# A written order for ScalarE and VectorE in the first stage of a transformer block kernel

## The chip, the cores and the metric

One core of a Trainium2 chip runs the whole program. The metric is device microseconds (us) of one execution; three executions of the kernel before gave 1308.18, 1308.55 and 1308.77 us. TensorE (PE in the profile) multiplies matrices into PSUM banks, ScalarE (ACT) and VectorE (DVE) work element by element, GpSimd (POOL) does a few small things, and DMA queues are fed by SyncE (SP), ScalarE and GpSimd.

## The reference

One layer of a hybrid block on 512 latent tokens of 2048 channels (256 context tokens beside them), all in float32:

```python
h = _modulate(_rmsnorm(xs, norm_g[l]), shift[:, None], scale[:, None])   # rmsnorm(x) * (1 + scale) + shift
p = h @ w_l                                   # 2048 -> 9216: q, k, v, z_a, u_b, z_b, g_a, g_b
q = _rope(_rmsnorm(_heads(p, OFF_Q, N_Q_HEADS), q_norm_g[l]), cos, sin) * q_scale
...
attn = _attention(q, jnp.concatenate([k, kc], axis=1), jnp.concatenate([v, vc], axis=1))
y_a = (attn * jax.nn.silu(z_a)) @ w_pa
y_b = (_fourier_mix(u_b) * jax.nn.silu(z_b)) @ w_pb
return (g_a * y_a + g_b * y_b) @ w_o          # then the gated residual and a last rmsnorm
```

`shift`, `scale` and `gate` are the product of `silu(c)` with `w_ada`. The change touches how `shift`, `scale` and `h` are made and how the first columns of `p` (u_b and z_b, 1024 of 9216) are computed beside that, and where two small tables for the rotations are loaded.

## The kernel before

Every float32 operand of a product is split into a high part `hi`, rounded to the format that TensorE multiplies fast, and the rest `lo`. ScalarE makes `hi` (a copy with rounding, L176) and VectorE `lo` (source minus `hi`, L177). One product is then three matmuls into the same bank: high weight by high row (L327), high weight by low row or the other way round (L328), and the remaining cross term (L329).

*The first stage* (0 to about 141 us) goes over the 2048 channels in 16 blocks of 128. x lies transposed, channel on partition, as `xt`. First the root of the mean square of every token: squares on ScalarE (L522, L526) or VectorE (L524), sums on VectorE (L527) and on TensorE (L528), root and reciprocal (L532, L533), and `spread` (L539), four fp32 products that put the reciprocals on all partitions. Then for each block k: `matvec`, 16 fp32 matmuls of `silu(c)` by a piece of `w_ada` (L551); ScalarE copies the result out (`ado`, L563); TensorE transposes it (L567); VectorE reduces it to columns (L576) and makes `gain` (L577) and `shift` (L579). `make_h` makes the row block: VectorE multiplies x by gain and reciprocal root (L592), ScalarE adds the shift and rounds to the high row (L593), VectorE makes the low row (L594). For k of 8 and above `form_row` makes three small VectorE results from blocks k and k-8 (L602 to L604), used in the second stage.

Beside this runs `start_work`, the products of the row blocks with the columns of u_b and z_b, as a generator that yields after each tile; `some(n)` lets it do n tiles. A piece covers one to four blocks and up to eight tiles of 128 columns. Tiles 0 to 3 stay in four banks named `pb` through the whole stage. Tiles 4 to 7 go to banks named `pc`, of which there are **two slots, used in turn**: a third `pc` tile can start only when the first has been taken out, the fourth when the second has. Taking out is `keep`: a ScalarE copy for block 0 (L611), otherwise the VectorE addition part <- pc + part (L613). The weights of the pieces come by SyncE's queue and are split by `split_next`.

What sets the order: TensorE's instructions stand in the order in which the code is written (`manual_schedule` for TensorE alone). For ScalarE and VectorE a scheduler chooses an order among ready work; `behind(ins)` only says that what stands inside it comes after `ins`. All engines run their own line in order.

*The turn to the second stage* (141 to about 178 us). The Fourier mixing of u_b takes `part` through `halves`, `channels`, `positions` and `gate_b`, and GpSimd writes the result to DRAM as `b_d` (two DMAs, L803). After that the remaining columns of `p` are computed by a seven-product scheme on weights that arrive as chains `R` (GpSimd's DMAs add to them, L280) and on forms of the rows (`S`, `Z`), again split by L176 and L177. The rotation tables `qr` (L1007 and L1008, `load_rotations`, issued by ScalarE) lie in the memory in which `part` lay, so their load has to wait until the `b_d` transfers are done; `rotations` multiplies them (L1013).

## Time and profile before

| what | value |
|---|---|
| three executions | 1308.18, 1308.55, 1308.77 us |
| profiled execution | 1308.72 us, span 1306.9 us, mean granted TensorE clock 0.998 |
| PE busy | 1278.5 us, 98% of the span |
| DVE, ACT, POOL busy | 993.8, 684.4, 166.4 us |
| chain that ended last | PE 78%, DVE 9%, DMA 6%, issue 3%, ACT 3% |

A timeline row reads: start, duration (both us from the start of the span), engine, line of the kernel, operation, output<-inputs, shapes, and in square brackets how long the engine had stood idle just before and what released it. A row of the windows view has the stretch, its length, busy time (and count) of PE, PE's weight loads, DVE, ACT and POOL, the granted TensorE clock, the share of the DMA engines in use and GB/s. A row of the waits view has the waiting engine and line, what it waited for, and total time, number and longest.

### The profile page before, as it was taken

What the parts mean: (1) busy time and instruction counts of PE and PEld (TensorE: products, weight loads), DVE (VectorE), ACT (ScalarE), POOL (GpSimd) and SP (SyncE); (2) the same over time, 40 slices, a digit from 0 to 9 for tenths busy, and PEclk for the clock granted to TensorE, in tenths of its full rate; (3) what the DMA queues carried; (4) which work ended last, traced back from release to release, by engine and by line L of the source; (5) the groups of instructions that cost most, each with busy time, mean ns of one, the idle gap of its engine ahead of it and who ended that gap; (6) DMA issues with size and microseconds to landing.
All of it is one profiled execution on the core that took longest, in us unless ns stands there. A gap on an engine that the chain in (4) does not pass through costs nothing.

```text
span 1306.9 us, 17539 instructions
## 1 busy us (share of the span) xinstructions
PE 1278.5 (98%) x6522; PEld 1046.7 (80%) x6522; DVE 993.8 (76%) x1296; ACT 684.4 (52%) x1080; POOL 166.4 (13%) x218
## 2 busy tenths in 40 slices
PE   7999999999999999999999999999999999999997
PEld 3676887888888888888888888888888888888885
DVE  4666889979788787657777766688898867887676
ACT  5222645555556455444354554666666646464554
POOL 0000011110202101011021020012110212221210
PEclk9999999999999999999999999999999999999999
DMA  9998486898899888976869897568872899998985
GB/s 384 351 367 345 169 235 160 252 235 267 211 269 261 253 292 257 323 212 180 265 202 266 300 227 248 180 214 247 245 238 81 234 254 239 248 214 230 220 205 170
DMA packets 103718, 318.54 MB, mean 244 GB/s; under 512 B 9808, under 2 KB 33104, under 8 KB 99280
## 3 DMA queue, kind: packets, MB, share of 16 engines
q1 hardware_dynamic: 54480, 197.86, 42.0%
q0 software_dynamic: 26544, 96.49, 34.6%
q10 hardware_dynamic: 22608, 23.07, 5.2%
q8 instruction: 51, 0.84, 0.2%
q14 instruction: 35, 0.29, 0.1%
HBM read 283.30 MB, written 34.09 MB: 243 GB/s over the span
## 4 chain that ended last, share of the span: by engine, by line
PE 78%; DVE 9%; DMA 6%; issue 3%; ACT 3%; SPq 0%; ACTq 0%; POOL 0%; DVEq 0%; POOLq 0%
PE banks L327 10%; PE banks L328 10%; PE banks L329 10%; PE x L329 7%; PE x L328 7%; PE x L327 6%; PE y L329 6%; PE y L327 6%; PE y L328 5%; DVE wlo L177 3%; PE banks L1371 2%; PE pd L551 2%; DMA wr<-in_w_g 2%; DMA wr<-in_ctx_toks 1%; DVE s L177 1%
## 5 line engine op out<-in xcount | busy, mean ns | idle before, releaser
L176 ACT ACTIVATE whi<-R 128x1024 fp32r<-128x1024 f32 x138 | 145.1, 1058 | 138.0 <-PE banks L329 49.1
L177 DVE TENSOR_TENSOR wlo<-R,whi 128x1024 fp32r<-128x1024 f32 x138 | 167.6, 1221 | 58.7 <-ACT whi L176 58.3
L177 DVE TENSOR_TENSOR wlo<-wr,whi 128x1024 fp32r<-128x1024 f32 (+1 forms) x122 | 147.2, 1212 | 65.0 <-ACT whi L176 64.8
L176 ACT ACTIVATE whi<-wr 128x1024 fp32r<-128x1024 f32 (+1 forms) x122 | 127.5, 1050 | 108.4 <-PE y L329 35.1
L327 PE MATMUL banks<-whi,s 128*128 128x512 f32 x396 | 157.2, 397 | 2.1 <-DVE ev L938 1.5
L329 PE MATMUL banks<-whi,s 128*128 128x512 f32 x396 | 155.2, 392 | 0.0
L328 PE MATMUL banks<-wlo,s 128*128 128x512 f32 x396 | 155.2, 392 | 0.0
L328 PE MATMUL x<-wlo,s 128*128 128x512 f32 x356 | 138.7, 390 | 0.3 <-DVE wlo L177 0.3
L327 PE MATMUL x<-whi,s 128*128 128x512 f32 x356 | 138.9, 390 | 0.0
L329 PE MATMUL x<-whi,s 128*128 128x512 f32 x356 | 138.7, 390 | 0.0
L328 PE MATMUL y<-wlo,s 128*128 128x512 f32 x308 | 120.2, 390 | 0.9 <-DVE wlo L177 0.9
L329 PE MATMUL y<-whi,s 128*128 128x512 f32 x308 | 119.9, 390 | 1.0 <-DVE s L177 1.0
L327 PE MATMUL y<-whi,s 128*128 128x512 f32 x308 | 120.2, 390 | 0.4 <-DVE cxe L1091 0.4
L280 POOL DMA_DIRECT2D R<-in_w_g x64 | 55.9, 873 | 423.3 <-DVE wlo L177 271.3
L176 ACT ACTIVATE s<-wr 128x512 fp32r<-128x512 f32 (+2 forms) x95 | 61.1, 676 | 72.1 <-DMA wr<-in_w_g 22.0
L177 DVE TENSOR_TENSOR s<-wr,s 128x512 fp32r<-128x512 f32 (+2 forms) x95 | 68.0, 747 | 34.1 <-ACT s L176 33.4
L327 PEld LDWEIGHTS banks<-whi,s 128*128 128x128 f32 x396 | 74.5, 188 | 17.6 <-ACT whi L176 1.9
L329 PEld LDWEIGHTS banks<-whi,s 128*128 128x128 f32 x396 | 74.4, 188 | 15.5
L328 PEld LDWEIGHTS banks<-wlo,s 128*128 128x128 f32 x396 | 74.5, 188 | 14.0 <-DVE wlo L177 0.2
L328 PEld LDWEIGHTS x<-wlo,s 128*128 128x128 f32 x356 | 66.9, 188 | 14.5 <-DVE wlo L177 0.7
L329 PEld LDWEIGHTS x<-whi,s 128*128 128x128 f32 x356 | 66.8, 188 | 13.8
L327 PEld LDWEIGHTS x<-whi,s 128*128 128x128 f32 x356 | 66.9, 188 | 13.7
(292 smaller groups left out, 2816.6 us busy)
## 6 DMA issues: line engine op xcount, KB each, us to landing
wr<-in_w_g SPq DMA_DIRECT2D x128, 512.0 KB, 5.2
wa<-in_w_ss SPq DMA_DIRECT2D x32, 1024.0 KB, 8.2
R<-in_w_g POOLq DMA_DIRECT2D x64, 512.0 KB, 6.9
R<-in_w_g SPq DMA_DIRECT2D x32, 512.0 KB, 5.8
wr<-in_w_gate SPq DMA_DIRECT2D x32, 512.0 KB, 5.2
wr<-in_w_o SPq DMA_DIRECT2D x24, 512.0 KB, 7.6
R<-in_w_o POOLq DMA_DIRECT2D x24, 512.0 KB, 9.2
wr<-in_w_pab SPq DMA_DIRECT2D x20, 512.0 KB, 5.7
```

Of the source, the lines that this page charges most:

```text
L176: first = nc.scalar.activation(hi, src, ACT.Copy)
L177: return first, nc.vector.tensor_tensor(lo, src, hi.bitcast(F32), op=ALU.subtract)
L280: nc.gpsimd.dma_start(chain[e.pc], e.nxt, accum_op=ALU.add)
L327: nc.tensor.matmul(o, ah, bh, start=start, stop=False, skip_group_check=cont)
L328: nc.tensor.matmul(o, ah, bl, start=False, stop=False, skip_group_check=cont)
L329: nc.tensor.matmul(o, al, bh, start=False, stop=stop, skip_group_check=cont)
L551: nc.tensor.matmul(acc[32 * j : 32 * j + 32], c2[:, n, :], w[:, k, :], start=n < 4, stop=n >= KK - 4)
L1371: nc.tensor.transpose(tp[:, k * P : (k + 1) * P], p[:, k * P : (k + 1) * P], ident)
```

## The change

1. For blocks 0 to 13 ScalarE and VectorE too run in the order in which the code is written; the last two blocks stay as they were, with `behind`. The squares get one more on VectorE (q=14).
2. Blocks 0 to 5 make the row another way. `by_root` forms y = x * reciprocal root before the columns are known; then ScalarE makes the high row straight from y with scale and shift (`row_hi`), and VectorE makes v = y * gain and the low row (`row_lo`). `hold` and `release` put one take-out of a bank between the two. Blocks 6 to 13 keep `make_h`.
3. Splits of weights are written ahead of the columns of a block, and in blocks 6 to 13 the take-outs of a block's `pc` tiles come where `some` stands in the code.
4. For one-block pieces with t = 0 the first two tiles do their four products with the high row first and those with the low row after them. `spread` stands between the halves of `matvec(0)`, and block 1's `matvec` comes after four tiles in place of two.
5. The first load of the rotation tables is issued by GpSimd; the second stays with ScalarE.

The diff; of the loops that are replaced only the new form is shown, since the old one stands in the kernel above:

```diff
@@ -520,7 +520,7 @@
             two = hm_tile([P, 2, T], F32, name=uid("sq"))
             a, b = two[:, 0, :], two[:, 1, :]
             nc.scalar.activation(a, xt[:, q, :], ACT.Square)
-            if q in (4, 8, 10):
+            if q in (4, 8, 10, 14):
                 nc.vector.tensor_tensor(b, xt[:, q + 1, :], xt[:, q + 1, :], op=ALU.mult)
             else:
                 nc.scalar.activation(b, xt[:, q + 1, :], ACT.Square)
@@ -554,10 +554,14 @@
 
     two = {}
 
-    def modulate(kb):
+    def modulate(kb, meanwhile=lambda: None):
         two[kb] = bank2()
         for h in range(2):
             matvec(kb, h)
+        meanwhile()
+        return taken(kb)
+
+    def taken(kb):
         o = o_of[kb] = pap.tile([P, 256], F32, tag="ada_o", bufs=2, name=uid("ado"))
         wada.pop(kb)
         return nc.scalar.copy(o, two[kb][:, :256])
@@ -570,7 +574,6 @@
         sp, o = two.pop(kb)[:, 256:], o_of.pop(kb)
         turned(sp, o)
         if kb == 0:
-            rx0.append(spread(*norms))
             warm(3, o)
         r = pap.tile([P, 2, 2], F32, tag="ada_r", bufs=2, name=uid("adr"))
         nc.vector.tensor_reduce(r, sp.rearrange("p (h g r) -> p h r g", h=2, g=4)[:, :, 0:2, :], axis=AX.X, op=ALU.add)
@@ -579,12 +582,26 @@
         last = nc.vector.tensor_scalar(shift[:, kb, :], r[:, 0, :], bada[:, kb : kb + 1], None, op0=ALU.add)
         return last
 
-    rx0 = []
+    rx0, y_of = [], {}
 
     def rows_of(kb):
         if kb % 2 == 0:
             pairs.append([hm_tile([P, 2, T], F32R, name=uid(n)) for n in ("hh", "hl")])
         hhi[kb], hlo[kb] = (t[:, kb % 2, :] for t in pairs[-1])
+
+    def by_root(kb):
+        y = y_of[kb] = whole["S3", 0][:, 2 * (kb % 2) : 2 * (kb % 2) + 2, :].rearrange("p a c -> p (a c)")
+        nc.vector.tensor_tensor(y, xt[:, kb, :], rx if kb else rx0[0], op=ALU.mult)
+
+    def row_hi(kb):
+        rows_of(kb)
+        nc.scalar.activation(hhi[kb], y_of[kb], ACT.Identity, bias=shift[:, kb, 0:1], scale=gain[:, kb, 0:1])
+
+    def row_lo(kb):
+        v = xt[:, kb, :]
+        nc.vector.tensor_scalar(v, y_of.pop(kb), gain[:, kb, 0:1], None, op0=ALU.mult)
+        nc.vector.scalar_tensor_tensor(hlo[kb], v, shift[:, kb, 0:1], hhi[kb].bitcast(F32),
+                                       op0=ALU.add, op1=ALU.subtract)
 
     def make_h(kb):
         rows_of(kb)
@@ -603,9 +620,12 @@
         nc.vector.tensor_tensor(whole["S3", h][:, i, :], a[:, :256], a[:, 256:], op=ALU.subtract)
         nc.vector.scalar_tensor_tensor(whole["Z5", h][:, i, :], a[:, 256:], d, b[:, 256:], op0=ALU.add, op1=ALU.subtract)
 
-    finals = []
+    finals, held = [], []
 
     def keep(t, acc, kb, nk):
+        if held and held[0] is None:
+            held[0] = t, acc, kb, nk
+            return
         dst = pt(t)
         if kb == 0 or t < 4:
             nc.scalar.copy(dst, acc)
@@ -624,6 +644,18 @@
                 order = [[(i, k)] for k in range(nk) for i in range(nt)]
             elif nt == 8:
                 order = [order[i] for i in TURNS]
+            if t == 0 and nk == 1:
+                both = [(i, sums_u[i] if i < 4 else bank3(), slice(P * i, P * i + P)) for (i, _), in order[:2]]
+                for i, acc, c in both:
+                    nc.tensor.matmul(acc, wh[:, 0, c], hhi[kb], start=kb == 0 or i > 3, stop=False, skip_group_check=i < 4)
+                    nc.tensor.matmul(acc, wl[:, 0, c], hhi[kb], start=False, stop=False, skip_group_check=i < 4)
+                for i, acc, c in both:
+                    nc.tensor.matmul(acc, wh[:, 0, c], hlo[kb], start=False, stop=i > 3, skip_group_check=i < 4)
+                    if i > 3:
+                        keep(i, acc, kb, nk)
+                order = order[2:]
+                yield 3
+                yield 3
@@ -658,65 +690,110 @@
...
+    def hold():
+        held[:] = [None]
+
+    def release():
+        k = held.pop()
+        keep(*k)
+
+    E = mybir.EngineType
+    with tc.manual_schedule(engines={E.PE}):
         norms = token_norms()
...
+        two[0] = bank2()
+        matvec(0, 0)
+        rx0.append(spread(*norms))
+        matvec(0, 1)
+        with tc.manual_schedule(engines={E.Activation, E.DVE}):
             split_next()
+            nc.scalar.copy(rx, rx0[0])
+            by_root(0)
+            taken(0)
+            wada[2] = wada_load(2)
+            load_start()
+            columns(0)
+            row_hi(0)
+            row_lo(0)
             split_next()
...
+            by_root(1)
+            some(4)
+            modulate(1, split_next)
+            wada[3] = wada_load(3)
+            load_start()
             some(2)
...
+            columns(1)
+            row_hi(1)
+            row_lo(1)
             some(2)
...
+            for kb in range(1, 4):
+                k = kb + 1
+                some(2)
+                by_root(k)
+                if kb > 1:
+                    split_next()
+                modulate(k)
+                if kb < 3:
+                    wada[k + 2] = wada_load(k + 2)
+                    load_start()
+                if kb == 1:
+                    split_next()
+                hold()
+                some(2)
+                columns(k)
+                row_hi(k)
+                release()
+                row_lo(k)
+                if kb == 3:
+                    some(2)
+                    by_root(5)
+                    modulate(5)
+                    for k in (6, 7):
+                        wada[k] = wada_load(k)
+                        load_start()
+                    hold()
+                    some(2)
+                    columns(5)
+                    row_hi(5)
+                    release()
+                    row_lo(5)
+                else:
+                    some(4)
+            for kb in range(4, KK - 4, 2):
+                some(3)
                 split_next()
...
+                for i in range(2):
+                    k = kb + 2 + i
+                    if i:
+                        some(3)
+                        split_next()
+                    modulate(k)
+                    if k + 2 < KK:
+                        wada[k + 2] = wada_load(k + 2)
+                        for _ in range(2 if k + 2 == KK - 3 else 1):
+                            load_start()
+                    some(2 - i)
+                    columns(k)
+                    make_h(k)
                     if k >= 8:
                         form_row(k - 8)
...
                 if kb == KK - 6:
                     split_table(0)
                     split_from(get(("dftc", 0)), fch[:, 0, :], fch[:, 1, :])
                     load_start()
+                some(3)
+        for i in range(2):
+            k = KK - 2 + i
+            some(2)
+            modulate(k)
+            some(2 - i)
+            columns(k)
+            ins = make_h(k)
+            with behind(ins):
+                split_next()
+                form_row(k - 8)
+            if not i:
+                load_start()
+        some(1)
         some(8)
     may[0], asks[0] = 1 << 30, nc.sync
     while next(work):
@@ -1003,9 +1080,9 @@
     new_q = lambda: qr[:, :1024].rearrange("p (a h d) -> p a h d", a=2, h=4)
     turning = qr[:, 1024:].rearrange("p (a t d) -> p a t d", a=2, t=4)
 
-    def load_rotations(rows):
-        nc.scalar.dma_start(turning, rope)
-        nc.scalar.dma_start(new_q()[:, 0, 0:2, :], rows)
+    def load_rotations(rows, q):
+        q.dma_start(turning, rope)
+        q.dma_start(new_q()[:, 0, 0:2, :], rows)
@@ -1216,7 +1293,7 @@
         qs[h] = take((2, T), F32R)
-    load_rotations(qkg[:, 0:2, :])
+    load_rotations(qkg[:, 0:2, :], nc.gpsimd)
@@ -1247,7 +1324,7 @@
                 with tc.issue_after(last_split[-1][1].ins):
                     rotations(HD ** -0.5)
             elif (g, name) == (KV, "P1"):
-                load_rotations(qkg[:, 2:4, :])
+                load_rotations(qkg[:, 2:4, :], nc.scalar)
             elif (g, name) == (KV, "Q5"):
                 with tc.issue_after(last_split[-1][1].ins):
                     rotations(1.0)
```

How instructions move, at three places. Names in a row are the program's, with the number of the buffer: `pc_` is a bank of the two turning slots, `adr` the reduced columns, `s_` here a low row being made, `wlo` a split of weights.

VectorE around the columns of block 9, before:

```order
L576 TENSOR_REDUCE adr_815<-pd_780 128x4
L577 TENSOR_SCALAR gain<-adr_815,bsc_98,small 128x2
L579 TENSOR_SCALAR shift<-adr_815,small 128x2
L592 SCALAR_TENSOR_TENSOR xt<-xt,gain,rx 128x512
L613 TENSOR_TENSOR part<-pc_830,part 128x512
L594 SCALAR_TENSOR_TENSOR s_759<-xt,shift,s_758 128x512
L602 TENSOR_TENSOR d_826<-shift 128x1
L603 TENSOR_TENSOR S_67<-xt 128x256
L177 TENSOR_TENSOR wlo_823<-wr_665,whi_822 128x1024
L604 SCALAR_TENSOR_TENSOR Z_69<-xt,d_826 128x256
L613 TENSOR_TENSOR part<-pc_838,part 128x512
L613 TENSOR_TENSOR part<-pc_846,part 128x512
```

and after the change:

```order
L579 TENSOR_REDUCE adr_823<-pd_788 128x4
L580 TENSOR_SCALAR gain<-adr_823,bsc_98,small 128x2
L582 TENSOR_SCALAR shift<-adr_823,small 128x2
L609 SCALAR_TENSOR_TENSOR xt<-xt,gain,rx 128x512
L611 SCALAR_TENSOR_TENSOR s_767<-xt,shift,s_766 128x512
L619 TENSOR_TENSOR d_830<-shift 128x1
L620 TENSOR_TENSOR S_67<-xt 128x256
L621 SCALAR_TENSOR_TENSOR Z_69<-xt,d_830 128x256
L633 TENSOR_TENSOR part<-pc_834,part 128x512
L633 TENSOR_TENSOR part<-pc_842,part 128x512
L633 TENSOR_TENSOR part<-pc_850,part 128x512
L177 TENSOR_TENSOR wlo_868<-wr_673,whi_867 128x1024
```

The first take-out of a bank behind the columns (pc_830 before, pc_834 now) moved from ahead of the low row (L594, now L611) to behind the low row and all three rows of `form_row`; the split of weights moved behind the take-outs. Blocks 7, 11 and 13 move in the same way; block 7 has no `form_row`, and at block 13 the splits `fsq` and `fch` stand ahead of the take-outs too.

VectorE around the columns of block 2, before:

```order
L613 TENSOR_TENSOR part<-pc_366,part 128x512
L576 TENSOR_REDUCE adr_373<-pd_338 128x4
L577 TENSOR_SCALAR gain<-adr_373,bsc_98,small 128x2
L579 TENSOR_SCALAR shift<-adr_373,small 128x2
L592 SCALAR_TENSOR_TENSOR xt<-xt,gain,rx 128x512
L613 TENSOR_TENSOR part<-pc_389,part 128x512
L613 TENSOR_TENSOR part<-pc_397,part 128x512
L594 SCALAR_TENSOR_TENSOR s_378<-xt,shift,s_377 128x512
L613 TENSOR_TENSOR part<-pc_405,part 128x512
```

and after the change:

```order
L594 TENSOR_TENSOR S_67<-xt,rx 128x512
L177 TENSOR_TENSOR wlo_365<-wr_235,whi_364 128x1024
L579 TENSOR_REDUCE adr_377<-pd_339 128x4
L580 TENSOR_SCALAR gain<-adr_377,bsc_98,small 128x2
L582 TENSOR_SCALAR shift<-adr_377,small 128x2
L633 TENSOR_TENSOR part<-pc_371,part 128x512
L602 TENSOR_SCALAR xt<-S_67,gain 128x512
L603 SCALAR_TENSOR_TENSOR s_382<-xt,shift,s_381 128x512
L633 TENSOR_TENSOR part<-pc_390,part 128x512
L633 TENSOR_TENSOR part<-pc_398,part 128x512
L633 TENSOR_TENSOR part<-pc_403,part 128x512
```

The product by the reciprocal root (L594, into S_67) stands ahead of the columns now, and a split of weights too. Of the three take-outs around the old low row (L594), one stands ahead of the new low row (L603) and three behind it.

ScalarE at the first load of the rotation tables, before:

```order
L176 ACTIVATE whi_1639<-R_1282 128x1024
L1007 DMA qr<-in_rope 128x1024
L1008 DMA qr<-in_qkg 128x256
L176 ACTIVATE s_1655<-Z_69 128x1024
L176 ACTIVATE whi_1660<-R_1279 128x1024
```

and after the change:

```order
L176 ACTIVATE whi_1648<-R_1287 128x1024
L176 ACTIVATE s_1664<-Z_69 128x1024
L176 ACTIVATE s_1686<-Z_70 128x1024
L176 ACTIVATE whi_1669<-R_1284 128x1024
L176 ACTIVATE s_1759<-S_67 128x1024
```

and GpSimd, after the change (before, the five rows are the same without the two of `qr`):

```order
L880 DMA b_d<-part 128x1024 x2
L1084 DMA qr<-in_rope 128x1024
L1085 DMA qr<-in_qkg 128x256
L280 DMA R_1284<-in_w_g 128x1024
L280 DMA R_1285<-in_w_g 128x1024
```

The two loads left ScalarE's line and stand in GpSimd's, between the writes of `b_d` and the additions to the weight chains `R`.

More of the change, by code (lines that the diff above doesn't have):

```diff
@@ L659, in split_next @@
         e.raws = []
-    with tc.manual_schedule(engines={mybir.EngineType.PE}):
-        norms = token_norms()
-        modulate(0)
-        wada[2] = wada_load(2)
-        load_start()
-        columns(0)
-        ins = make_h(0)
-        nc.scalar.copy(rx, rx0[0])
-        split_next()
-        with behind(ins):
-            split_next()
-            split_next()
-        for kb in range(4):
+    def hold():
[3 more added lines that the diff above has]
+        keep(*k)
@@ L674, in block_kernel @@
             some(2)
-            modulate(kb + 1)
-            if kb < 3:
-                wada[kb + 3] = wada_load(kb + 3)
-                load_start()
+            columns(1)
+            row_hi(1)
+            row_lo(1)
             some(2)
-            columns(kb + 1)
-            ins = make_h(kb + 1)
-            with behind(ins):
-                split_next()
-            if kb == 3:
-                some(2)
-                modulate(5)
-                for k in (6, 7):
-                    wada[k] = wada_load(k)
-                    load_start()
-                some(2)
-                columns(5)
-                make_h(5)
-            else:
-                some(4)
@@ L695, in block_kernel @@
-        for kb in range(4, KK - 2, 2):
-            n = 3 if kb < KK - 4 else 2
-            for i in range(2):
-                k = kb + 2 + i
-                some(n)
-                modulate(k)
-                if k + 2 < KK:
-                    wada[k + 2] = wada_load(k + 2)
-                    for _ in range(2 if k + 2 == KK - 3 else 1):
-                        load_start()
-                some(2 - i)
-                columns(k)
-                ins = make_h(k)
-                with behind(ins):
-                    split_next()
+            for kb in range(1, 4):
[31 more added lines that the diff above has]
+                    some(4)
@@ L710, in block_kernel @@
                     if k >= 8:
                         form_row(k - 8)
-                if k == KK - 2:
-                    load_start()
-            some(n - (n == 2))
-            with behind(ins):
                 if kb == KK - 6:
```

## The prediction

> **What bounds the kernel now.** I read the windows view first, by stage, then the waits of PE, then the timelines of PE and DVE at each place that the order of the changed kernel moves.

> ```profile
> 0.00:20.00 20.00, 11.51 (x48) 4.25 (x48) 10.10 (x22) 12.27 (x22) 1.89 (x11) 1.00 0.91 363
> 20.00:60.00 40.00, 36.49 (x279) 23.77 (x275) 22.69 (x42) 12.74 (x20) 0.00 (x0) 1.00 0.92 362
> 60.00:141.00 81.00, 80.40 (x590) 57.06 (x591) 52.43 (x109) 25.30 (x38) 0.00 (x0) 1.00 0.86 332
> 170.00:240.00 70.00, 67.32 (x292) 53.98 (x291) 64.28 (x76) 38.18 (x57) 9.73 (x12) 1.00 0.77 210
> ```

> PE sets the pace. From 20 to 60 us it stands idle 40.00 - 36.49 = 3.5 us, from 60 to 141 only 0.6, from 170 to 240 2.7. The granted clock is 1.00 throughout, so PE's work is neither longer nor shorter after the change: only its idle time can move. What the change can save is bounded by the first and the last of these; the long middle stretch has nothing to give and can only lose.

> ```profile
> PE pb L328 <- DVE s L594: 2.0, 4, 1.2
> PE pb L327 <- ACT s L593: 0.9, 2, 0.6
> ```

> These are the early waits: six times PE waits for a high row or for a low row of a new block.

> **The late blocks: where the change loses.** In blocks 7, 9, 11 and 13 VectorE's order changes from product, *take-out of a bank*, low row, ... to product, low row, the rows of `form_row`, *take-out*. PE's fourth `pc` tile after the transposes needs the slot that this take-out frees. First the price of being released by it, which block 13 shows already:

> ```profile
> 122.48 0.39 PE L329 MATMUL pc<-s,wlo 128*128 128x512 f32 x1
> 123.47 0.50 PE L327 MATMUL pc<-s,whi 128*128 128x512 f32 x1 [0.60 <-DVE part L613]
> ...
> 120.53 0.17 DVE L576 TENSOR_REDUCE adr<-pd 128x4 f32<-128x16 f32 x1
> 122.73 1.28 DVE L613 TENSOR_TENSOR part<-pc,part 128x512 f32<-128x512 f32 x2
> 125.99 1.22 DVE L177 TENSOR_TENSOR fsq<-wr,fsq 128x1024 fp32r<-128x1024 f32 x1
> 127.12 0.42 DVE L177 TENSOR_TENSOR fch<-wr,fch 128x256 fp32r<-128x256 f32 x1
> 127.46 1.22 DVE L177 TENSOR_TENSOR wlo<-wr,whi 128x1024 fp32r<-128x1024 f32 x1
> ```

> The take-out starts at 122.73 and PE, which had waited 0.60, goes on at 123.47, 0.74 after that start; its first matmul after a stop takes 0.50 and not 0.39, so a stop costs its wait and 0.1.

> Block 7, without `form_row`:

> ```profile
> 73.73 0.16 DVE L576 TENSOR_REDUCE adr<-pd 128x4 f32<-128x16 f32 x1
> 74.25 0.75 DVE L592 SCALAR_TENSOR_TENSOR xt<-xt,gain,rx 128x512 f32<-128x512 f32 x1
> 75.80 0.75 DVE L594 SCALAR_TENSOR_TENSOR s<-xt,shift,s 128x512 fp32r<-128x512 f32 x1 [0.20 <-ACT s L593]
> 76.47 0.68 DVE L613 TENSOR_TENSOR part<-pc,part 128x512 f32<-128x512 f32 x1
> 75.91 0.39 PE L327 MATMUL pc<-s,whi 128*128 128x512 f32 x1
> ```

> The low row waited for ScalarE (0.20), so it cannot start earlier when the take-out leaves its place ahead of it. The take-out then starts where the next instruction stood, 76.47, and PE's fourth tile at 76.47 + 0.74 = 77.21 against 75.91: 1.3 + 0.1 = **1.4 us**.

> Blocks 9 and 11 have `form_row` in between:

> ```profile
> 89.33 0.17 DVE L576 TENSOR_REDUCE adr<-pd 128x4 f32<-128x16 f32 x1
> 91.40 0.75 DVE L594 SCALAR_TENSOR_TENSOR s<-xt,shift,s 128x512 fp32r<-128x512 f32 x1 [0.19 <-ACT s L593]
> 92.47 1.22 DVE L177 TENSOR_TENSOR wlo<-wr,whi 128x1024 fp32r<-128x1024 f32 x1
> 93.61 0.48 DVE L604 SCALAR_TENSOR_TENSOR Z<-xt,d 128x256 f32<-128x256 f32 x1
> 94.00 1.28 DVE L613 TENSOR_TENSOR part<-pc,part 128x512 f32<-128x512 f32 x2
> 91.51 0.39 PE L327 MATMUL pc<-s,whi 128*128 128x512 f32 x1
> ...
> 104.93 0.17 DVE L576 TENSOR_REDUCE adr<-pd 128x4 f32<-128x16 f32 x1
> 107.11 0.39 PE L327 MATMUL pc<-s,whi 128*128 128x512 f32 x1
> ```

> Low row and the two small rows end where the split stood, 92.47; Z takes 94.00 - 93.61 = 0.39 more. The take-out starts at 92.86, PE at 93.60 against 91.51: 2.1 + 0.1 = **2.2**. Block 11 has the same distances (reduction to fourth tile 2.18 in both): **2.2**.

> Block 13: in the new order no split stands behind the reduction, so low row and `form_row` end as in block 9, 92.86 - 89.33 = 3.53 after it, at 124.06. Then come `fsq` (127.12 - 125.99 = 1.13) and `fch` (0.34): take-out at 125.53, PE at 126.27, against 123.47 now: **2.8**, its 0.1 being paid before too. Sum 1.4 + 2.2 + 2.2 + 2.8 = **8.6 us**. What would be late next, the next piece's split, was made one piece earlier. From both sides: at most the same sum plus 0.3 at each place if ScalarE's high row waits behind a split, 9.8; at least 6.2, if the reduction comes 0.6, one take-out, earlier each time.

> **The early blocks: a gain.** Block 2 shows the chain that is shortened:

> ```profile
> 39.46 0.17 DVE L576 TENSOR_REDUCE adr<-pd 128x4 f32<-128x16 f32 x1
> 40.77 0.72 ACT L593 ACTIVATE s<-xt,shift 128x512 fp32r<-128x512 f32 x1 [3.05 <-DVE xt L592]
> 42.45 0.74 DVE L594 SCALAR_TENSOR_TENSOR s<-xt,shift,s 128x512 fp32r<-128x512 f32 x1
> 43.24 0.50 PE L328 MATMUL pb<-s,whi 128*128 128x512 f32 x1 [1.20 <-DVE s L594]
> ```

> From the reduction to the high row's start 1.31 are spent; the product's 0.67 (its pitch as block 7's rows give it, 75.80 to 76.47 for an operation of the same kind) goes away, since y is ready, so the columns are done 0.52 after the reduction (73.73 to 74.25 in block 7) and ScalarE starts. VectorE has one take-out meanwhile (about 0.6, half of the pair at 122.73), then v = y * gain, then the low row. The new v has no row of its shape; bounds are 0 if it lay wholly under ScalarE's high row and 0.67, the pitch of L592 on 128x512 with two tensors, if it took as long. I take 0.67, since it reads the same 128x512 elements. The low row then starts 0.52 + 0.6 + 0.67 = 1.8 after the reduction in place of 2.99: 1.2 sooner, of which the moved split ahead of the reduction (over a microsecond, as 92.47 to 93.61 above) takes back about half.

> [...]

> Counting all six waits with pitch and refill, PE loses 4.3 here now: 2.0 + 0.9, and some 0.23 at each of six stops (0.1 refill, the rest the modelled end of the matmul before). I keep 1.8 of it. Half a microsecond is block 0's, where `spread` now stands ahead of the second half of `matvec` and waits for the reciprocal:

> ```profile
> 18.64 0.95 DVE L533 RECIPROCAL s<-s 128x128 f32<-128x128 f32 x1 [2.77 <-ACT s L532]
> 19.05 1.07 PE L551 MATMUL pd<-wa,c 128*32 128x256 f32 x16 [0.96 <-DMA wa<-in_w_ss]
> ```

> PE takes that half up at 19.05 now, and will only after 19.59 and four fp32 products. The rest is 0.4 at block 1, 0.8 at block 2 and its last tile, 0.1 at block 3. Gain **2.5**, between 1.5 and 4.3. The square that went to VectorE is worth nothing: in the window from 0 to 20 neither engine is full, and PE's sums of the squares end that stretch.

> **The turn, 141 to 170 us.** ScalarE and VectorE stand in a slightly different order here: a split of a weight chain and one more product of `gate_b` stand ahead of the first low part of `channels`.

> ```profile
> 153.49 1.88 DVE L177 TENSOR_TENSOR al<-pb,ah 128x512 fp32r<-128x512 f32 x3
> ```

> PE takes the first of these three up with no reserve; one more product of 128x512 ahead of it (0.6 in pitch) and up to 0.6 from ScalarE's split make a new stop: **0.9**, between 0 and 1.2.

> **The second stage: a gain.** ScalarE's line stands still behind the load of the tables, which waits for `b_d` to land:

> ```profile
> 169.73 6.70 DMA b_d<-part
> ...
> 176.58 0.38 ACTq L1007 DMA_DIRECT2D qr<-in_rope  x1
> ...
> 178.58 1.23 DVE L177 TENSOR_TENSOR s<-Z,s 128x1024 fp32r<-128x1024 f32 x1 [3.54 <-ACT s L176]
> 181.00 0.50 PE L328 MATMUL y<-wlo,s 128*128 128x512 f32 x1 [0.94 <-DVE wlo L177]
> 181.25 0.90 POOL L280 DMA_DIRECT2D R<-in_w_g  x1 [10.97 <-DVE wlo L177]
> 190.61 1.29 DVE L1013 SCALAR_TENSOR_TENSOR qr<-qr 128x512 f32<-128x512 f32 x2
> ```

> With the load in GpSimd's line ScalarE goes on near 172.5, and VectorE, idle 3.54 before 178.58, starts its forms about 3.5 earlier. PE's stop at 181.00 goes, and the three small ones up to 228 with it, since VectorE runs without a gap from 178 to 190 and beyond and its lead is kept. All four are the 2.7 idle of the window plus pitch and refill, 3.8 together; I take **3.3**, down to 1.5 if part of the lead is lost to weights that have not come. What waits behind the tables in GpSimd's line are the additions to `R`: the first is issued at 181.25 now, would be ready some 3.5 earlier, and stands behind two issues of about 0.9 from 176.5 on: some 178.3, still earlier than now. The tables land about 7 us after their issue if they take what `b_d` took (6.70), at 184, ahead of 190.61 less the lead (187.1). Cost nothing; if they came 3.5 late, the lead would be lost.

> **Sum** against the profiled execution (1308.72, which is the span and 1.8 around it): - 2.5 + 8.6 + 0.9 - 3.3 = + 3.7, to which the last two blocks add about 0.1 by a changed start: 1312.5. The profiled execution lies 0.17 over the median of 1308.55, so **1312.4 us** for a median.

> **The rivals.**

> *All ends good.* Both gains come in full (3.2 early, 3.8 in the second stage), the turn costs 0.4, the late blocks 7.5: + 0.9, **1309.5**. For it: VectorE is only 65% busy from 60 to 141 us and could run ahead. Against it: its low row waits for ScalarE, so running ahead does not help the take-out.

> *The take-out does not hold PE* (the other side). If the fourth tile's slot is one that is free long before, for instance because the slots are handed out by release and not in turn, the 8.6 fall away whole: - 2.5 + 0.9 - 3.3, **1303.8**. It decides as soon as the late loss is below 4.9. Against it stands the row at 123.47: PE there waited for a take-out behind the reduction by name.

> *The second stage gives nothing.* GpSimd's line delays additions or tables, or the lead ends at the next weights: + 7.0, **1315.7**. For it: DMA queues are 0.77 busy in that window; against it the margin of 3 us above.

> *The clock falls.* At block 13 PE stands idle about 0.8 + 2.8 = 3.6 us. This case shows a longer stop without a lower clock:

> ```profile
> PE pd L528 <- DVE s L527: 7.5, 2, 7.1
> ```

> with 1.00 granted in its window. [...] If half speed held for as long as the stop, 3.6 us, PE would lose 1.8: **1314.2**.

> **How the numbers follow.** Forecast 0.62, all ends good 0.18, no hold 0.06, second stage without gain 0.11, clock 0.03. The forecast's own range is 1310.5 to 1314.5. The range 1309.0 to 1316.0 takes in all but the side without a hold and the tails. A change under 0.2% (2.6 us: 1305.9 to 1311.2) cannot be told from none: into it fall "all ends good" and 0.07 of the forecast, 0.25; faster 0.06; slower 0.69.

> **What would show it.** PE rows of L327 with a wait for `part` L633 of 1.1 to 1.3 us at block 7, near 2 at 9 and 11 and 3.5 at 13, and PE idle of about 8.5 us between 60 and 141: if they are missing, the main term is wrong. The first `pb` matmul near 24.1; no stop over 0.6 after block 1 for a low row but at block 2. A wait for `al` near 155. VectorE without the 3.54 gap, no stop of PE at 181, ScalarE past 172 without a DMA in its line, the tables landed before L1090 asks for them.

## The result, and the profile after

The changed kernel takes 1315.26 us (median of 6, 1313.68 to 1320.26) against 1308.5 (median of 6) for the kernel before: ratio 1.0055, 95% interval 1.0038 to 1.0072, so 5 to 9 us slower. Its profiled execution took 1314.17 us, with a span of 1312.4, 5.5 over the one before.

The windows view of the changed kernel, with the columns as before, and its row of PE's waits for a take-out:

```profile
20.00:60.00 40.00, 38.48 (x298) 25.23 (x297) 24.81 (x48) 13.77 (x21) 0.00 (x0) 1.00 0.96 381
60.00:141.00 81.00, 72.59 (x516) 49.71 (x515) 44.82 (x94) 18.80 (x28) 0.00 (x0) 0.96 0.78 309
170.00:240.00 70.00, 69.49 (x341) 58.68 (x341) 67.96 (x82) 37.59 (x57) 11.76 (x15) 1.00 0.74 205
PE pc L327 <- DVE part L633: 8.4, 4, 3.4
```

PE's idle time from 20 to 60 us fell from 3.5 to 1.5, from 170 to 240 from 2.7 to 0.5, and from 60 to 141 it rose from 0.6 to 8.4. The clock in that middle stretch, 1.00 before, is 0.96. These four stops make up the 8.4 (PE's timeline):

```profile
75.38 0.50 PE L327 MATMUL pc<-s,whi 128*128 128x512 f32 x1 [1.14 <-DVE part L633]
93.21 0.50 PE L327 MATMUL pc<-s,whi 128*128 128x512 f32 x1 [1.93 <-DVE part L633]
111.03 0.50 PE L327 MATMUL pc<-s,whi 128*128 128x512 f32 x1 [1.93 <-DVE part L633]
...
126.56 0.39 PE L329 MATMUL pc<-s,wlo 128*128 128x512 f32 x1
130.36 0.79 PE L327 MATMUL pc<-s,whi 128*128 128x512 f32 x1 [3.41 <-DVE part L633]
130.95 0.63 PE L328 MATMUL pc<-s,whi 128*128 128x512 f32 x1
131.37 0.63 PE L329 MATMUL pc<-s,wlo 128*128 128x512 f32 x1
```

All four are the first matmul of the fourth `pc` tile in blocks 7, 9, 11 and 13. Behind the last the same matmul takes 0.63 and follows the one before it after 0.42, not 0.23: the clock is at half, from 129.71 to 136.53, as finer windows show (the figure behind the five busy times; the last section says why the windows are cut so):

```profile
126.29:129.70 3.41, 0.66 (x3) 0.19 (x2) 3.02 (x7) 1.60 (x3) 0.00 (x0) 1.00 0.99 412
129.71:133.12 3.41, 2.76 (x7) 2.19 (x8) 1.19 (x2) 0.00 (x0) 0.00 (x0) 0.50 0.95 322
133.12:136.53 3.41, 3.41 (x15) 2.01 (x17) 0.69 (x1) 0.00 (x0) 0.00 (x0) 0.50 0.20 79
136.53:139.94 3.41, 3.41 (x38) 2.21 (x31) 0.00 (x0) 0.37 (x1) 0.00 (x0) 1.00 0.02 5
```

How far the changed kernel's PE is behind (+) or ahead (-) of the kernel before can be read at one event after another, since PE's work is the same: the start of a block's transposition (L567, now L571), the first matmul into `x`, and so on, after minus before.

| event | before, us | after, us | behind | what lies between |
|---|---|---|---|---|
| block 0's transposition | 20.70 | 22.23 | +1.53 | `spread` now ahead of it |
| first `pb` matmul | 23.60 | 24.30 | +0.70 | shorter way to the high row |
| block 2 | 38.65 | 37.61 | -1.04 | block 1 without its stops |
| block 4 | 56.36 | 54.53 | -1.83 | blocks 2 and 3 |
| block 7 | 72.92 | 71.09 | -1.83 | |
| block 8 | 82.76 | 82.36 | -0.40 | stop of block 7, +1.43 |
| block 10 | 98.36 | 100.19 | +1.83 | stop of block 9, +2.23 |
| block 12 | 113.96 | 118.04 | +4.08 | stop of block 11, +2.25 |
| block 14 | 129.79 | 139.48 | +9.69 | stop of block 13 and the clock, +5.61 |
| first matmul into `x` | 168.52 | 178.43 | +9.91 | the turn, +0.22 |
| third product begins | 192.02 | 200.22 | +8.20 | no stop at 181 |
| L329 into `y` after a stop | 227.60 | 233.99 | +6.39 | two of three small stops gone, one halved |
| end of the span | 1306.9 | 1312.4 | +5.5 | |

Of the 5.61 at block 13, the stop itself accounts for 2.81: from 126.56 to 130.36 are 3.80, against 123.47 - 122.48 = 0.99 before. The other 2.80 are work at half clock.

VectorE's line at block 9 shows why PE stops (timeline of the changed kernel):

```profile
91.00 0.75 DVE L611 SCALAR_TENSOR_TENSOR s<-xt,shift,s 128x512 fp32r<-128x512 f32 x1 [0.79 <-ACT s L610]
91.67 0.15 DVE L619 TENSOR_TENSOR d<-shift 128x1 f32<-128x1 f32 x1
91.74 0.42 DVE L620 TENSOR_TENSOR S<-xt 128x256 f32<-128x256 f32 x1
92.08 0.48 DVE L621 SCALAR_TENSOR_TENSOR Z<-xt,d 128x256 f32<-128x256 f32 x1
92.47 1.28 DVE L633 TENSOR_TENSOR part<-pc,part 128x512 f32<-128x512 f32 x2
```

VectorE waits 0.79 for ScalarE's high row, with the take-out that it could do meanwhile standing four rows further down its line. Before, that wait was 0.19, because the take-out filled it. The take-out starts at 92.47, PE at 93.21: 0.74, the distance read at block 13 of the kernel before.

In the second stage ScalarE runs on and GpSimd holds the tables' loads (timelines of ScalarE and GpSimd; `b_d` of this run lands at about 185.9):

```profile
181.38 1.06 ACT L176 ACTIVATE whi<-R 128x1024 fp32r<-128x1024 f32 x1 [7.82 <-PE x L329]
182.35 1.99 ACT L176 ACTIVATE s<-Z 128x1024 fp32r<-128x1024 f32 x2
...
185.97 0.54 POOL L1084 DMA_DIRECT2D qr<-in_rope  x1 [5.78 <-DMA b_d<-part]
186.50 0.55 POOL L1085 DMA_DIRECT2D qr<-in_qkg  x1
187.41 0.89 POOL L280 DMA_DIRECT2D R<-in_w_g  x1 [0.36 <-DVE wlo L177]
```

The addition to `R` waits for its split and not for the tables: by its 0.36 the queue was free before. `L1090`, which reads the tables, starts at 197.38 without a wait.

### The profile page after: what moved, and what is told of

Its sections match the earlier page's. It is cut to its first block, busy times and chain, and to the rows that moved or that the text cites. A ratio compares the mean times of both kernels' runs of the same rounds, so it can differ in the third digit from the quotient of the medians.

```text
span 1312.4 us, 17551 instructions
## 1 busy us (share of the span) xinstructions
PE 1279.8 (98%) x6522; PEld 1047.6 (80%) x6522; DVE 997.4 (76%) x1303; ACT 684.9 (52%) x1079; POOL 167.8 (13%) x220
## 4 chain that ended last, share of the span: by engine, by line
PE 91%; DVE 4%; ACT 2%; issue 1%; DMA 1%; SPq 0%; ACTq 0%; DVEq 0%
PE banks L327 10%; PE banks L328 10%; PE banks L329 10%; PE x L329 9%; PE x L328 9%; PE x L327 9%; PE y L329 7%; PE y L327 7%; PE y L328 7%; PE banks L1448 2%; PE pd L551 2%; PE pb L327 2%; PE pb L329 1%; PE pb L328 1%; PE pc L327 1%
## 5 line engine op out<-in xcount | busy, mean ns | idle before, releaser
L176 ACT ACTIVATE whi<-R 128x1024 fp32r<-128x1024 f32 x138 | 145.7, 1058 | 142.2 <-PE banks L329 53.5
L177 DVE TENSOR_TENSOR wlo<-R,whi 128x1024 fp32r<-128x1024 f32 x138 | 167.8, 1221 | 57.0 <-ACT whi L176 56.7
L177 DVE TENSOR_TENSOR wlo<-wr,whi 128x1024 fp32r<-128x1024 f32 (+1 forms) x122 | 147.3, 1212 | 63.6 <-ACT whi L176 63.0
L176 ACT ACTIVATE whi<-wr 128x1024 fp32r<-128x1024 f32 (+1 forms) x122 | 127.5, 1050 | 114.3 <-PE y L329 37.9
L327 PE MATMUL banks<-whi,s 128*128 128x512 f32 x396 | 157.0, 397 | 2.4 <-DVE ev L1015 1.5
L329 PE MATMUL banks<-whi,s 128*128 128x512 f32 x396 | 155.1, 392 | 0.0
L328 PE MATMUL banks<-wlo,s 128*128 128x512 f32 x396 | 155.1, 392 | 0.0
L327 PE MATMUL x<-whi,s 128*128 128x512 f32 x356 | 138.8, 390 | 0.0
L328 PE MATMUL x<-wlo,s 128*128 128x512 f32 x356 | 138.5, 389 | 0.0
L329 PE MATMUL x<-whi,s 128*128 128x512 f32 x356 | 138.5, 389 | 0.0
L329 PE MATMUL y<-whi,s 128*128 128x512 f32 x308 | 119.8, 389 | 0.5 <-DVE s L177 0.5
L327 PE MATMUL y<-whi,s 128*128 128x512 f32 x308 | 120.0, 389 | 0.2 <-DVE cxe L1168 0.2
L328 PE MATMUL y<-wlo,s 128*128 128x512 f32 x308 | 119.8, 389 | 0.0
L280 POOL DMA_DIRECT2D R<-in_w_g x64 | 56.0, 874 | 418.7 <-DVE wlo L177 261.1
L176 ACT ACTIVATE s<-wr 128x512 fp32r<-128x512 f32 (+2 forms) x95 | 61.1, 675 | 66.2 <-DMA wr<-cf_d 16.1
L177 DVE TENSOR_TENSOR s<-wr,s 128x512 fp32r<-128x512 f32 (+2 forms) x95 | 67.9, 747 | 28.8 <-ACT s L176 28.0
L327 PEld LDWEIGHTS banks<-whi,s 128*128 128x128 f32 x396 | 74.4, 188 | 17.9 <-ACT whi L176 1.9
L329 PEld LDWEIGHTS banks<-whi,s 128*128 128x128 f32 x396 | 74.4, 188 | 15.4
L328 PEld LDWEIGHTS banks<-wlo,s 128*128 128x128 f32 x396 | 74.5, 188 | 14.0 <-DVE wlo L177 0.2
L328 PEld LDWEIGHTS x<-wlo,s 128*128 128x128 f32 x356 | 66.8, 188 | 13.9 <-DVE wlo L177 0.2
L329 PEld LDWEIGHTS x<-whi,s 128*128 128x128 f32 x356 | 66.8, 188 | 13.9
L327 PEld LDWEIGHTS x<-whi,s 128*128 128x128 f32 x356 | 66.8, 188 | 13.8
```

What stands on the lines that cost most here:

```text
L176: first = nc.scalar.activation(hi, src, ACT.Copy)
L177: return first, nc.vector.tensor_tensor(lo, src, hi.bitcast(F32), op=ALU.subtract)
L280: nc.gpsimd.dma_start(chain[e.pc], e.nxt, accum_op=ALU.add)
L327: nc.tensor.matmul(o, ah, bh, start=start, stop=False, skip_group_check=cont)
L328: nc.tensor.matmul(o, ah, bl, start=False, stop=False, skip_group_check=cont)
L329: nc.tensor.matmul(o, al, bh, start=False, stop=stop, skip_group_check=cont)
```

## The experiments

Two chips took part in the experiments; each kernel is compared with the kernel before on its own chip. The first four ran on one chip, the rest on another.

**Take-out between product and low row.**

```diff
-    def make_h(kb):
+    def make_h(kb, meanwhile=lambda: None):
...
         act = nc.scalar.activation(hhi[kb], v, ACT.Identity, bias=shift[:, kb, 0:1])
+        meanwhile()
...
-                    make_h(k)
+                    make_h(k, (lambda: some(1)) if i else (lambda: None))
...
-                some(3)
+                some(2)
```

> The changed kernel, but in blocks 7, 9, 11 and 13 the take-out of the second pc tile is written between the product (L609) and the low row, as VectorE had it before. Theory (the four late stops come from this place in VectorE's line, and the lower clock follows from the longest of them): the stops of 1.4, 2.2, 2.2 and 3.8 us and the 2.8 us of the lower clock go, 12.4 us less than the profiled 1314.2: 1301.8, clock 1.00 between 60 and 141 us. Rival (the lower clock has a cause of its own): 1304.6 with a clock below 1.00 again. Rival (the stops follow from something else in the new order): no less than 1313.

Measured: 1304.58 us against 1309.78, ratio 0.9959 (0.9946 to 0.9971). Its windows row and VectorE's line at block 9:

```profile
60.00:141.00 81.00, 81.00 (x596) 57.90 (x595) 53.70 (x110) 26.46 (x39) 0.00 (x0) 1.00 0.86 330
...
89.09 0.68 DVE L634 TENSOR_TENSOR part<-pc,part 128x512 f32<-128x512 f32 x1
89.97 0.75 DVE L612 SCALAR_TENSOR_TENSOR s<-xt,shift,s 128x512 fp32r<-128x512 f32 x1 [0.20 <-ACT s L610]
```

PE is busy for the whole 81 us and the clock is 1.00: every late stop is gone, the one that the kernel before had at block 13 too, and with them the lower clock. The place of one VectorE instruction per block is the cause. The time is 5.2 under the kernel before, not 6.7. Part of the lead is given back later, in waits that the profile before did not have or had shorter:

```profile
428.11 0.50 PE L328 MATMUL x<-wlo,s 128*128 128x512 f32 x1 [1.76 <-DVE wlo L177]
...
918.43 0.61 PE L327 MATMUL banks<-whi,s 128*128 128x512 f32 x1 [4.09 <-DVE R L1397]
```

The profiled execution took 1310.0, the other five 1302.66 to 1304.99, so a wait as long as the second is hardly in those. Behind the second the clock fell too: that matmul takes 0.61, and 0.99 is granted from 800 to 1100 us, where the kernels of the other experiments have 1.00. What makes these two late was not tried.

**Only the tables' queue.** The kernel before with one call changed:

```diff
-    load_rotations(qkg[:, 0:2, :])
+    load_rotations(qkg[:, 0:2, :], nc.gpsimd)
```

> The kernel before with one edit: the first load of the rotation tables goes to GpSimd's queue. Theory (ScalarE's line was held by that load, and its lead is kept): the stop of 1.3 us at 181 goes and most of the 2.5 us in the stops at 222 to 228: 3.4 less, 1305.1. Rival (the gain in the second stage needs the other order of ScalarE and VectorE at the turn): within 0.5 us of 1308.5.

Measured: 1306.77 against 1309.78, ratio 0.9978 (0.9969 to 0.9987), 3.0 less. By the same events as in the table, the third product begins 1.7 earlier relative to the first matmul into `x` (+0.15 there, -1.56 at the third product). The queue alone gives a gain of that size; the order at the turn is not needed for it.

**The splits of block 13 behind the take-outs.**

```diff
+                some(3)
                 if kb == KK - 6:
                     split_table(0)
                     split_from(get(("dftc", 0)), fch[:, 0, :], fch[:, 1, :])
                     load_start()
-                some(3)
```

> The changed kernel, but at block 13 the splits fsq and fch stand behind the take-outs. The stop of PE there falls from 3.8 to 2.3 us, 1.5 less in any case. Theory (the clock falls because PE stood idle for so long): no lower clock, another 2.8 less, 1309.9. Rival (the clock falls for another reason): 1312.7, clock again about 0.96 between 60 and 141 us.

Measured: 1313.47 against 1309.78, ratio 1.0036 (1.0024 to 1.0048). The stop at block 13 fell as both expected, and the clock behind it stayed up (matmuls of 0.39 to 0.40 from 130.95 on); but the clock of the whole stretch is 0.98, because it now fell behind block 9 (seven matmuls of 0.63 from 94.96 on). The three stops of PE:

```profile
93.34 0.50 PE L327 MATMUL pc<-s,whi 128*128 128x512 f32 x1 [1.94 <-DVE part L633]
112.79 0.50 PE L327 MATMUL pc<-s,whi 128*128 128x512 f32 x1 [1.94 <-DVE part L633]
130.62 0.50 PE L327 MATMUL pc<-s,whi 128*128 128x512 f32 x1 [1.94 <-DVE part L633]
```

From 93.34 to 112.79 are 19.45 us, in the changed kernel 111.03 - 93.21 = 17.82: 1.63 more for the same work, behind a stop that cost nothing extra there. So my theory, that the longest stop lowers the clock, fell here: of three stops of 1.94, one was caught.

**The stop filled.** Block 14's `matvec` once more ahead of block 13's fourth tile (the extra result is not used):

```diff
-                some(3)
+                    some(2)
+                    two[14] = bank2()
+                    matvec(14, 0)
+                    matvec(14, 1)
+                    some(1)
+                else:
+                    some(3)
```

> The changed kernel, with the 32 matmul records of block 14's matvec (about 1.9 us of PE work) done once more ahead of the fourth pc tile of block 13, into a bank that nobody reads. VectorE's line is as it was, so the fourth tile starts no earlier. Theory (idle time of PE lowers the clock): the longest stretch without PE work falls to about 1.9 us, the clock stays at 1.00, 2.8 less than the changed kernel: 1311.4. Rival (something else lowers the clock): no change, 1314.2.

Measured: 1317.05 against 1309.78, ratio 1.0057 (1.0045 to 1.0069). Neither reading came out:

```profile
111.11 0.50 PE L327 MATMUL pc<-s,whi 128*128 128x512 f32 x1 [1.94 <-DVE part L633]
...
128.53 1.93 PE L551 MATMUL pd<-wa,c 128*32 128x256 f32 x32
132.01 0.50 PE L327 MATMUL pc<-s,whi 128*128 128x512 f32 x1 [1.54 <-DVE part L633]
```

With 1.93 of work in it, the stop left the clock alone (blocks 13 to 14 cost 2.80 over the kernel before, the stop's own 2.81). But now the clock fell behind block 11 (matmuls of 0.63 from 112.70 to 115.26; 3.84 there, where the changed kernel lost 2.25), behind a stop of 1.94. As a test of what filling one stop brings it is inconclusive, since another stop took the fall.

**The changed kernel again.**

> The changed kernel unedited, beside the next three on one chip. Theory (a stop of about 2 us or more can lower the clock, and which of the four stops does is not fixed): slower than the kernel before by 5.5 to 8 us, the clock below 1.00 behind one stop or two, not always block 13's. Rival (only the stop of 3.8 us lowers it): 5.5 to 6.5 us slower, behind block 13 alone.

Measured: 1316.18 against 1309.52, ratio 1.0042 (1.0028 to 1.0057). The profile of the same program, run again:

```profile
93.23 0.50 PE L327 MATMUL pc<-s,whi 128*128 128x512 f32 x1 [1.94 <-DVE part L633]
...
94.36 0.63 PE L328 MATMUL pc<-s,whi 128*128 128x512 f32 x1
...
97.69 0.40 PE L327 MATMUL pb<-s,whi 128*128 128x512 f32 x1
...
112.68 0.50 PE L327 MATMUL pc<-s,whi 128*128 128x512 f32 x1 [1.94 <-DVE part L633]
131.97 0.80 PE L327 MATMUL pc<-s,whi 128*128 128x512 f32 x1 [3.40 <-DVE part L633]
```

Here the clock fell twice: about 0.9 us after the stop of block 9 had ended, for some 3.4 us (0.63 from 94.36, 0.40 again at 97.69), and at block 13. Block 9's stop with what follows cost 3.85 in place of 2.23, block 13's 4.24 in place of 5.61. The same program, the same stops, another price: which stop is caught is not fixed by the program alone (the last section shows where the falls lay).

**One stop left, at block 13, and one left, at block 9.** The first experiment's kernel with one block excepted:

```diff
-                    make_h(k, (lambda: some(1)) if i else (lambda: None))
+                    make_h(k, (lambda: some(1)) if i and k != 13 else (lambda: None))
...
-                some(2)
+                some(3 if k == 13 else 2)
```

> The kernel with the take-out between product and low row, but not at block 13, whose order is that of the changed kernel: one stop of 3.8 us is left. Both theories: the clock falls behind it, 3.8 + 2.8 = 6.6 us over the kernel with no such stop (5.2 under the kernel before, so 1.4 over it). If the fall of the clock needs several stops in a row: 3.8 over, 1.4 under the kernel before, clock as in the kernel before.

> The same, but only block 9 keeps the order of the changed kernel: one stop of 2.2 us is left. Theory (stops of 2 us lower the clock in some executions): 2.2 us over the kernel without stops in some, 3.5 to 5 in others, about 2 under the kernel before; the profile shows a clock below 1.00 behind 93 us or not. Rival (only longer stops do): 3.0 under the kernel before, the clock 1.00 between 60 and 141 us.

Measured: block 13 alone 1309.08 against 1309.52, ratio 0.9985 (0.9972 to 0.9998); block 9 alone 1305.62, ratio 0.9964 (0.9948 to 0.9979). The stop and the windows row with one stop at block 13:

```profile
125.32 0.50 PE L327 MATMUL pc<-s,whi 128*128 128x512 f32 x1 [3.40 <-DVE part L634]
...
60.00:141.00 81.00, 77.20 (x577) 54.14 (x576) 50.87 (x107) 23.72 (x35) 0.00 (x0) 1.00 0.81 318
```

A stop of 3.40, as long as in the changed kernel, and no lower clock in this execution: the stop cost its 2.81 over the kernel before and nothing more. Both theories had expected a fall there, and both were wrong; the last section shows how this stop lay. Block 9's stop of 1.94 was not caught either in its profile (1.00 granted from 60 to 141 us). Against the kernel without stops (5.2 under the kernel before, on the other chip) the medians are 4.8 over at block 13 (0.4 under the kernel before) and 1.3 over at block 9 (3.9 under), where the lengths of the stops alone say 3.8 and 2.2. The medians are not fine enough to say in how many executions the clock fell.

**A stop twice as long.**

```diff
                     if k >= 8:
-                        form_row(k - 8)
+                        for _ in range(6 if k == 13 else 1):
+                            form_row(k - 8)
```

> As the kernel with one stop at block 13, but form_row of that block is done six times in place of once (same results each time), which holds the take-out 4.0 us longer: a stop of some 7.8 us. Theory (the clock falls when an idle stretch happens to cover a window that runs on its own time, so a stop of 2 to 4 us is caught sometimes and one of twice that always): the profile shows a clock below 1.00 and matmul pitches of 0.43 behind the stop, 4.0 plus 1.5 to 3 over the kernel with one stop. Rival (idle length does not matter, the fall comes by chance or from the DMA load): 4.0 over it and the clock as in it.

Measured: 1313.29 against 1309.28, ratio 1.0031 (1.0019 to 1.0042), by the differences to the kernel before 4.4 over the kernel with one stop. In the profile:

```profile
128.70 0.79 PE L327 MATMUL pc<-s,whi 128*128 128x512 f32 x1 [7.40 <-DVE part L634]
...
128.50:134.00 5.50, 5.30 (x16) 3.84 (x19) 1.44 (x3) 0.00 (x0) 0.00 (x0) 0.53 0.49 191
```

The clock fell, as expected, and block 13 cost 9.10 over the kernel before, of which 2.81 + 4.0 are the stop and 2.3 the clock. The one profile agrees with the theory; the medians, at 4.4 over, do not separate it from the rival, since the kernel with a single stop may itself be caught in some of its runs.

**The tables back in ScalarE's line, in the changed kernel.**

```diff
-    load_rotations(qkg[:, 0:2, :], nc.gpsimd)
+    load_rotations(qkg[:, 0:2, :], nc.scalar)
```

> The changed kernel with the first load of the rotation tables back in ScalarE's line. Theory (the queue alone makes the gain in the second stage): a stop of PE near 191 us again and small ones behind it, 3 to 4 us over the changed kernel, 9 to 11 over the kernel before. Rival (the written order at the turn has part in it): 1 to 2 over the changed kernel.

Measured: 1318.27 against 1309.28, ratio 1.0070 (1.0052 to 1.0087): 9.0 over the kernel before, 2.3 more than the changed kernel's 6.7 on that chip. The stop is back:

```profile
191.16 0.50 PE L328 MATMUL y<-wlo,s 128*128 128x512 f32 x1 [0.63 <-DVE wlo L177]
```

It is 0.63 long, 0.94 before, and the three small stops behind it return at full length. In the same profile the clock falls behind the stops of blocks 9 and 13 (matmuls of 0.63 from 94.97 and from 132.95 on), as in the changed kernel run again. By the medians the edit costs 2.3, by the ratios (1.0070 - 1.0042) 3.7: between the two expectations and within the theory's by the second reckoning, with intervals too wide to choose. With the 3.0 of the kernel before plus the tables alone, the queue is worth 2 to 4 us in either surrounding.

**Both repairs.** The take-out moved as in the first experiment, and `spread` behind both halves of the first `matvec`:

```diff
         matvec(0, 0)
-        rx0.append(spread(*norms))
         matvec(0, 1)
+        rx0.append(spread(*norms))
...
+            taken(0)
             nc.scalar.copy(rx, rx0[0])
             by_root(0)
-            taken(0)
```

> The take-out between product and low row in all four blocks, and spread behind both halves of the first matvec (and ScalarE's copy of its result ahead of the copy of rx). Theory (spread's wait for the reciprocal holds the second half of matvec): the first pb matmul comes near 23.4 us in place of 24.7, and the lead at block 7 is 2.2 to 2.7 us in place of 1.4 (as that chip has it); 5.5 to 6.5 under the kernel before. Rival (the wait for x's and w_ada's transfers sets the start): first pb matmul within 0.3 of 24.7.

Measured: 1302.94 us (1302.14 to 1303.76) against 1309.52, ratio 0.9936 (0.9918 to 0.9954), 6.6 less: the fastest of all. PE's start:

```profile
19.01 1.07 PE L551 MATMUL pd<-wa,c 128*32 128x256 f32 x16 [0.87 <-DMA wa<-in_w_ss]
20.02 1.16 PE L539 MATMUL pc<-s 128*128 128x128 f32 x8
...
23.95 0.50 PE L651 MATMUL pb<-s,whi 128*128 128x512 f32 x1 [1.27 <-ACT s L598]
```

The second half of `matvec` starts at 19.01 again (20.66 in the changed kernel), and the first `pb` matmul at 23.95, not the 23.4 expected. The transposition follows `spread` at 21.01 (20.70 in the kernel before); but on VectorE `by_root` (L594) now stands ahead of the reduction to columns and waits for ScalarE's copy of `rx` until 21.83, so that the reduction starts at 22.43 (21.22 in the kernel before), and the high row, which PE waits for, late with it. The lead at block 7 is 2.15, a little under what was expected.

## Why the prediction was right, point by point

The direction was right, and so was the main term with its mechanism. The size was short: +3.9 was forecast and +6.8 measured (medians). The 1315.26 us lie above the forecast's own range, 1310.5 to 1314.5, and only inside the wider one, which ends at 1316.0. In the profiled execution the excess is the clock, which the prediction had given 0.03. Two prices of rivals lie near by coincidence: 1315.7 for "the second stage gives nothing", although the second stage did gain, and 1314.2 for the clock, which the profiled 1314.17 meets because the clock cost 1.0 more than that and 0.9 was gained elsewhere.

*Late blocks.* The main term was right in each part: 1.4, 2.2, 2.2 and 2.8 were predicted, 1.43, 2.23, 2.25 and 2.81 are measured. The chain that gave them (the low row cannot move ahead because ScalarE's high row holds it, the take-out starts where the next instruction stood, PE follows 0.74 later) stands row for row in the trace, and moving that one instruction back removes all four stops.

*Early blocks.* 2.5 predicted, 1.83 measured (table, block 4). The term was mis-sized at the start: PE's second half of `matvec` was held to 20.66, and the first `pb` matmul came 0.70 later, not 0.5. The sum also counted the stop of 0.30 just ahead of that matmul, 0.5 with its restart, as gained; that does not go with a first `pb` matmul half a microsecond later, and without it the sum would have been 2.0. Block 2's part came as weighed, with no stop for a low row and one of 0.42 for a take-out:

```profile
38.82 0.17 DVE L579 TENSOR_REDUCE adr<-pd 128x4 f32<-128x16 f32 x1
...
39.35 0.68 DVE L633 TENSOR_TENSOR part<-pc,part 128x512 f32<-128x512 f32 x1
39.95 0.48 DVE L602 TENSOR_SCALAR xt<-S,gain 128x512 f32<-128x512 f32 x1
40.53 0.75 DVE L603 SCALAR_TENSOR_TENSOR s<-xt,shift,s 128x512 fp32r<-128x512 f32 x1
```

The low row starts 1.7 after the reduction (1.8 predicted, 2.99 before). The new v takes 0.48 and its pitch is 0.58, where I took 0.67. The 0.67 was the pitch of a product of two tensors; of 128x512 such a product (L594) takes 0.68 in this trace, 1.4 times the 0.48 of the new v (L602).

*The turn.* 0.9 predicted, 0.22 measured. The mechanism is there, a small stop ahead of the first matmul that reads `al`, but the term was mis-sized: 0.9 was taken from a product and a split that both stand ahead of it, but VectorE's first low part starts at 163.42, 153.49 before: 9.93 later, where PE is 9.69 behind, so 0.24 of it is left. It was inside the bounds given.

*Second stage.* 3.3 predicted; the events give 9.91 - 6.39 = 3.5 up to 234 us, and another 0.9 by the end that I did not follow. Alone it is worth 3.0 (1.7 to 4.1 by its interval).

*The clock.* Here the prediction gave a chance of 0.03, and it happened, in the profiled execution at the price of 2.80, not 1.8. No run shows half speed for 3.6 us, which that price took; the trace shows 0.50 for 6.82 us (129.71 to 136.53). Without the clock the terms sum to -1.83 + 8.72 + 0.22 - 3.5 = +3.6, the forecast's +3.7, and the profiled time would be about 1312.3; that the two agree so well is in part luck, since the misses of the early blocks and of the turn, 0.7 each, cancel. With the clock and the 0.9 it is +5.5. The median of the six executions lies another 1.1 above the profiled one; what they spent there no trace shows.

The step that failed is the reading of one row: the stop of 7.1 us in the first 20 us, with 1.00 in the windows row, was taken as a sign that idle time does not lower the clock. The trace of the kernel before has no record of the clock ahead of 11.48 us, so the 1.00 says nothing about the stretch behind that stop. The matmuls there do: the first ones of L528 start at 8.12, 8.98, 9.83 and 10.68, 0.85 us apart, and those from 11.51 on (11.51, 11.94, 12.37) 0.43 apart. PE was at half speed behind the stop, so the row was no evidence against the rival, although it does not tell whether the stop or the start of the program was the reason. In the changed kernel the clock did fall behind a stop of 3.41, and in its second profile behind one of 1.94 too (last section).

The other rivals fell: the take-out did hold PE, the second stage did gain, and the late blocks cost 8.7 and not the 7.5 of "all ends good".

## What to carry to other kernels

When an engine's line is written out by hand, look at what stands behind each instruction that waits for another engine: a short instruction that frees a buffer belongs into the wait, not behind it. Price the move by the row that stood next in the line and by the distance from freeing to reuse, both read from the trace; it came out to a few hundredths here. And keep each stop of TensorE short: in these profiles one of 1.1 us never lowered the clock (0 of 5), one of 1.9 us sometimes did (4 of 12), and one of 3.4 us mostly (3 of 4), at 1.4 to 2.8 us beside its length.

## What the runs showed of the hardware that was not expected

A stop of the same length lowered the clock in one place and not in another. Over the eight profiles that have such stops, those of 1.1 us (block 7) were caught in none of 5 (twice the changed kernel, and three kernels with its block 7); those of 1.9 us in 4 of 12; those of 3.4 us in 3 of 4; the one of 7.4 us was caught. A fall cost 1.4 to 2.8 us. The same program was caught at block 13 alone in one execution and at blocks 9 and 13 in another.

```profile
90.76:94.17 3.41, 1.47 (x7) 0.91 (x6) 2.75 (x6) 1.18 (x2) 0.00 (x0) 1.00 0.97 405
94.17:97.58 3.41, 3.41 (x10) 2.62 (x9) 1.82 (x2) 0.00 (x0) 0.00 (x0) 0.50 0.07 28
...
120.33:123.73 3.40, 1.58 (x7) 0.94 (x6) 2.61 (x6) 1.98 (x3) 0.00 (x0) 1.00 1.02 423
123.73:127.14 3.41, 1.82 (x8) 1.51 (x9) 2.26 (x5) 0.00 (x0) 0.00 (x0) 1.00 0.82 281
```

The shorter stop lay whole in one window, which was idle for 1.94, and the next window ran at half. The longer one was divided between two windows, 1.82 and 1.58 idle, and the clock stayed up. The kernel before and the changed kernel, cut like this from the first change to the end of PE's work, agree with it: the changed kernel has one window at full clock that was idle for more than 1.80 us, block 13's with 2.75 idle (126.29 to 129.70, above), and that one alone was followed by one at half. Its stops of 1.93 were divided, block 9's into 0.88 and 1.05, block 11's into 0.13 and 1.80, and not caught; in the kernel before no window was idle for more than 1.32. Of the windows at half, that of the changed kernel in which PE was busy for 2.76 us was followed by another; its second, busy for 3.41, and the two of the run again, busy for 3.41 and 3.15, were the last. So the changed kernel, whose stop at block 13 ran 0.65 into the first low window, paid for two. If a stop of 1.94 is caught only when it lies whole in one window, that is at 3.41 - 1.94 = 1.47 of 3.41 positions, 0.43 of them (an estimate from these lengths; 4 of 12 were). None of the windows named here was idle for a time between 1.82 and 1.94, so what that does is not shown.
